# One FFN half of each kind, gate and up as a 2x2 block product of seven products

## Chip, cores and metric

The kernel runs on one core of one Trainium2 chip. The metric is device microseconds (us) of one execution; lower is better. The engines named below are TensorE (PE, with its weight loads as PEld), VectorE (DVE), ScalarE (ACT), GpSimd (POOL) and SyncE (SP), which issues most DMAs.

## What is computed

One decoder layer on 1024 tokens of width 1024 in float32: half a SwiGLU FFN, a mixer of two kinds of heads, half a SwiGLU FFN again, a final norm. Cut to what the change touches (D_FF is 2816 = 22 x 128):

```python
def rms_norm(x, g):
    return x * lax.rsqrt(jnp.mean(x * x, axis=-1, keepdims=True) + NORM_EPS) * g

def swiglu(h, w_gate, w_up, w_down):
    return (jax.nn.silu(h @ w_gate) * (h @ w_up)) @ w_down

x = x + 0.5 * swiglu(rms_norm(x, ffn1_norm), ffn1_w_gate, ffn1_w_up, ffn1_w_down)   # FFN1
x = x + hybrid_mixer(rms_norm(x, mix_norm), ...)
x = x + 0.5 * swiglu(rms_norm(x, ffn2_norm), ffn2_w_gate, ffn2_w_up, ffn2_w_down)   # FFN2
return rms_norm(x, final_norm)
```

## The kernel before

Tokens are cut into two halves of 512 (`TB`); activations lie feature-major, so that a tile is 128 features by 512 tokens. The order of the work is: FFN1 and the mixer's input projection of half 0 (`front`, L841), the mixer of half 0, FFN1 and input projection of half 1, the mixer of half 1, then for each half the output projection (`project_out`) and FFN2 (loop at L882 to L887). The mixer of a half is woven by the scheduler into the matmuls of what follows it. FFN1 of the first half runs before any mixer work exists, FFN2 of the second half after all of it.

**Precision.** A float32 product is made of three matmuls in the faster type fp32r: every operand is split into `hi` (a cast on ACT, L64) and `lo` (the rest, a subtraction on DVE, L65), and `mm3` (L89) adds hi x hi, hi x lo and lo x hi into one PSUM tile, per 128 rows of the contraction.

**FFN** (`ffn`, L172). `gain_split` (L153) makes the input h = x times the norm's gain, as eight hi/lo pairs `h_hi`, `h_lo`; the factor of the norm itself, r (`rs`), is computed beside the first products and multiplied in afterwards. The 22 columns of 128 gate and up weights are done in groups of 4, 4, 4, 4, 3, 3 (`GROUPS`). For each column `product` (L182) loads and splits the 1024x128 weights of gate, then of up, in two pieces of 128x512 each (`load_piece`, L69: DMA into `w_raw`, split into `w_hi`, `w_lo`), and runs 8 x 3 matmuls of 512 tokens into a PSUM tile. `gate` (L188) makes a = silu(gate r) r up: two products on DVE, silu on ACT, a product with the up tile on DVE, and a split into `a_hi`, `a_lo`. After each group the down products run (L230 to L235): for each of 8 output rows one piece of weights, 3 matmuls per column of the group, and an update of x on DVE. The first gate product of the next group is placed ahead of them (L229), so that PE has work while the last a is made.

In the second half of FFN2 the last group ends differently: `Finish` (L238) makes the down products token-major and goes straight on to the final norm and the output.

**What sets the order.** The program is written for a scheduler that places instructions on each engine's queue by priority and by readiness in its own model, and gives out buffers; every engine then works its queue in that order. What stands under `high_priority(AHEAD)` is drawn ahead: loads, splits, reads of PSUM. Buffers come from pools (L826 to L830), and a tile waits until the one that had its buffer is done: 5 raw weight tiles (`wraw`), 3 pairs of split weights (`whl`), 4 scratch tiles (`ft`); in PSUM 3 + 2 + 2 + 1 banks (`psf`, `hq`, `rq`, `ry`). The tiles `ra`, `bkt`, `uv` (pool `rw`) and `t4` belong to the mixer.

The input projection holds one place that the prediction uses: `tokens` (L313) multiplies with 256 columns at a time, with a new stationary operand for each matmul (L325 to L327).

Of the kernel before, what the change touches and what calls it, by code (L numbers as in the profile page):

```python
# [51 lines left out]
class Half:  # L52


    def __init__(self, hi, lo):
# [30 lines left out]
    return out  # L86


def mm3(E, ps, pairs, at=None, hook=None):  # L89
    n = len(pairs)  # L90
    for i, (w, x) in enumerate(pairs):
        if i == at:
            hook()
        E.nc.tensor.matmul(ps, w.hi, x.hi, start=(i == 0), stop=False)  # L94
        E.nc.tensor.matmul(ps, w.hi, x.lo, start=False, stop=False)  # L95
        E.nc.tensor.matmul(ps, w.lo, x.hi, start=False, stop=(i == n - 1))  # L96


def psum(E):
# [69 lines left out]
    return out  # L169


def ffn(E, xs, g, wgu, wdn, r=None, finish=None):  # L172
# [15 lines left out]
    def gate(pg, pu, half):  # L188
        with E.tc.high_priority(AHEAD):
            s = E.ft.tile([P, TB], F32, name="ft")  # L190
            if normed:
                nc.scalar.activation(out=s, in_=pg, func=AF.Silu)
            else:
                nc.vector.tensor_tensor(out=s, in0=pg, in1=r, op=ALU.mult)  # L194
                nc.scalar.activation(out=s, in_=s, func=AF.Silu)  # L195
                nc.vector.tensor_tensor(out=s, in0=s, in1=r, op=ALU.mult)  # L196
# [6 lines left out]
            return split(E, s, hi, lo)  # L203

    late = []
    for f0, nf in GROUPS:
# [23 lines left out]
        for d in range(KD):  # L230
            w = load_w(E, wdn[d, :, f0 * P:(f0 + nf) * P], nf)
            p = E.psf.tile([P, TB], F32, name="psf")
            mm3(E, p, list(zip(w, a)))
            with E.tc.high_priority(AHEAD):
                nc.vector.scalar_tensor_tensor(out=xs[d], in0=p, scalar=0.5, in1=xs[d], op0=ALU.mult, op1=ALU.add)  # L235
# [736 lines left out]
```

## Time and profile before

| what | value |
|---|---|
| median of 3 runs | 2111.35 us (2110.51 to 2111.99) |
| the profiled execution | 2111.92 us |
| its span, first to last instruction | 2109.9 us |
| first half of FFN1 in the span | about 7 to 373 us |
| second half of FFN2 in the span | about 1740 us to the end |
| instructions | 30312 |

The page of the profile gives, for each engine, busy time and its share of the span, and below it 40 slices of the span (52.7 us each) with the busy share of each engine in tenths. A group of instructions is shown by line, engine, operation and operands, with count, busy time and mean length. Matmuls and DVE instructions overlap their neighbours by some part, so lengths add up to more than the span; distances between starts do not have this flaw. For this reading, the slices of the two engines that the change loads:

```profile
DVE  7444445635888757766634788958784776444554
ACT  5223323626765445434626775546533553322333
```

Slices 1 to 7 are the first half of FFN1 and the last seven the second half of FFN2: DVE stands at 4 to 5 tenths there, ACT at 2 to 3, while the slices between, with the mixer woven in, reach 8 and 9 on DVE.

### The profile page before, as it was taken

What the parts mean: (1) busy time and instruction counts of PE and PEld (TensorE: products, weight loads), DVE (VectorE), ACT (ScalarE), POOL (GpSimd) and SP (SyncE); (2) the same over time, 40 slices, a digit from 0 to 9 for tenths busy, and PEclk for the clock granted to TensorE, in tenths of its full rate; (3) what the DMA queues carried; (4) which work ended last, traced back from release to release, by engine and by line L of the source; (5) the groups of instructions that cost most, each with busy time, mean ns of one, the idle gap of its engine ahead of it and who ended that gap; (6) DMA issues with size and microseconds to landing.
All of it is one profiled execution on the core that took longest, in us unless ns stands there. A gap on an engine that the chain in (4) does not pass through costs nothing.

```text
span 2109.9 us, 30312 instructions
## 1 busy us (share of the span) xinstructions
PE 2088.7 (99%) x11286; PEld 1698.6 (81%) x11286; DVE 1337.3 (63%) x2272; ACT 963.0 (46%) x1540; POOL 34.5 (2%) x68
## 2 busy tenths in 40 slices
PE   8999999999999999999999999999999999999998
PEld 6888888988888778877988878877787788888887
DVE  7444445635888757766634788958784776444554
ACT  5223323626765445434626775546533553322333
POOL 2000000010000000000000000000000000000000
PEclk9999999999999999999999999999999999999999
DMA  4333334544334423332644433423332453333332
GB/s 151 96 97 99 95 90 120 186 147 155 117 119 120 110 78 107 102 96 82 211 155 155 153 111 110 116 81 106 108 98 72 140 182 97 97 98 95 98 114 68
DMA packets 162724, 244.34 MB, mean 116 GB/s; under 512 B 37616, under 2 KB 57072, under 8 KB 162576
## 3 DMA queue, kind: packets, MB, share of 16 engines
q1 hardware_dynamic: 161712, 241.04, 38.4%
q8 instruction: 89, 1.46, 0.3%
q10 hardware_dynamic: 864, 1.36, 0.2%
q14 instruction: 59, 0.48, 0.1%
HBM read 210.35 MB, written 31.98 MB: 115 GB/s over the span
## 4 chain that ended last, share of the span: by engine, by line
PE 96%; DVE 1%; DMA 1%; issue 1%; ACT 1%; SPq 0%; DVEq 0%; ACTq 0%
PE psf L95 27%; PE psf L96 27%; PE psf L94 27%; PE rq L559 2%; PE rq L648 1%; PE hq L95 1%; PE hq L96 1%; PE hq L94 1%; PE rq L641 1%; PE rq L652 1%; PE ry L645 0%; DMA w_raw<-in_wgu_dram 0%; PE rq L639 0%; PE hq L485 0%; PE hq L478 0%
## 5 line engine op out<-in xcount | busy, mean ns | idle before, releaser
L64 ACT CAST w_hi<-w_raw 128x512 fp32r<-128x512 f32 (+2 forms) x696 | 420.5, 605 | 862.8 <-PE psf L95 763.8
L96 PE MATMUL psf<-h_hi,w_lo 128*128 128x512 f32 x1840 | 720.6, 392 | 0.5 <-DVE w_lo L65 0.5
L95 PE MATMUL psf<-h_lo,w_hi 128*128 128x512 f32 x1840 | 721.0, 392 | 0.0
L94 PE MATMUL psf<-h_hi,w_hi 128*128 128x512 f32 x1840 | 720.6, 392 | 0.3 <-ACT w_hi L64 0.3
L65 DVE TENSOR_TENSOR w_lo<-w_raw,w_hi 128x512 fp32r<-128x512 f32 (+2 forms) x696 | 460.9, 665 | 236.2 <-ACT w_hi L64 231.1
L96 PEld LDWEIGHTS psf<-h_hi,w_lo 128*128 128x128 f32 x1840 | 345.4, 188 | 73.6 <-DVE w_lo L65 1.5
L94 PEld LDWEIGHTS psf<-h_hi,w_hi 128*128 128x128 f32 x1840 | 345.5, 188 | 73.4 <-issue 1.2
L95 PEld LDWEIGHTS psf<-h_lo,w_hi 128*128 128x128 f32 x1840 | 345.4, 188 | 72.7 <-issue 0.7
L95 PE MATMUL psf<-a_lo,w_hi 128*128 128x512 f32 x680 | 268.3, 395 | 0.0
L96 PE MATMUL psf<-a_hi,w_lo 128*128 128x512 f32 x680 | 267.3, 393 | 0.0
L94 PE MATMUL psf<-a_hi,w_hi 128*128 128x512 f32 x680 | 266.7, 393 | 0.5 <-ACT a_hi L64 0.5
L235 DVE SCALAR_TENSOR_TENSOR x<-psf,x 128x512 f32<-128x512 f32 x184 | 126.1, 687 | 131.6 <-PE psf L96 130.9
L95 PEld LDWEIGHTS psf<-a_lo,w_hi 128*128 128x128 f32 x680 | 127.6, 188 | 28.1 <-issue 1.4
L94 PEld LDWEIGHTS psf<-a_hi,w_hi 128*128 128x128 f32 x680 | 127.6, 188 | 27.9 <-ACT a_hi L64 1.5
L96 PEld LDWEIGHTS psf<-a_hi,w_lo 128*128 128x128 f32 x680 | 127.7, 188 | 26.5 <-issue 0.5
L200 DVE TENSOR_TENSOR ft<-psf,ft 128x512 f32<-128x512 f32 x83 | 57.0, 687 | 71.3 <-PE psf L96 71.0
L194 DVE TENSOR_TENSOR ft<-psf,rs 128x512 f32<-128x512 f32 x64 | 44.1, 689 | 69.1 <-PE psf L96 69.0
L64 ACT CAST a_hi<-ft 128x512 fp32r<-128x512 f32 x88 | 54.5, 620 | 37.7 <-DVE ft L200 32.3
L65 DVE TENSOR_TENSOR a_lo<-ft,a_hi 128x512 fp32r<-128x512 f32 x88 | 60.3, 687 | 7.3 <-ACT a_hi L64 3.7
L386 DVE TENSOR_TENSOR ev<-psf,rs 128x512 f32<-128x512 f32 x44 | 30.3, 690 | 54.3 <-PE psf L96 54.3
L196 DVE TENSOR_TENSOR ft<-ft,rs 128x512 f32<-128x512 f32 x66 | 45.4, 691 | 8.4 <-ACT ft L195 4.6
L195 ACT ACTIVATE ft<-ft 128x512 f32<-128x512 f32 x66 | 41.5, 632 | 18.2 <-DVE ft L194 18.0
(332 smaller groups left out, 1966.7 us busy)
## 6 DMA issues: line engine op xcount, KB each, us to landing
w_raw<-in_wgu_dram SPq DMA_DIRECT2D x352, 256.0 KB, 3.1
w_raw<-in_wd_dram SPq DMA_DIRECT2D x134, 256.0 KB, 2.7
w_raw<-in_win_dram SPq DMA_DIRECT2D x96, 256.0 KB, 2.8
w_raw<-in_wd_dram SPq DMA_DIRECT2D x56, 192.0 KB, 2.3
w_raw<-in_wout_dram SPq DMA_DIRECT2D x32, 256.0 KB, 2.9
park<-x SPq DMA_DIRECT2D x16, 256.0 KB, 3.6
x<-park SPq DMA_DIRECT2D x16, 256.0 KB, 3.9
ft<-od SPq DMA_DIRECT2D x16, 256.0 KB, 3.3
```

The costliest lines, as they stand in the source:

```text
L64: nc.scalar.copy(out=hi, in_=raw)
L65: nc.vector.tensor_tensor(out=lo, in0=raw, in1=f32(hi), op=ALU.subtract)
L94: E.nc.tensor.matmul(ps, w.hi, x.hi, start=(i == 0), stop=False)
L95: E.nc.tensor.matmul(ps, w.hi, x.lo, start=False, stop=False)
L96: E.nc.tensor.matmul(ps, w.lo, x.hi, start=False, stop=(i == n - 1))
L194: nc.vector.tensor_tensor(out=s, in0=pg, in1=r, op=ALU.mult)
L195: nc.scalar.activation(out=s, in_=s, func=AF.Silu)
L196: nc.vector.tensor_tensor(out=s, in0=s, in1=r, op=ALU.mult)
L200: nc.vector.tensor_tensor(out=s, in0=pu, in1=s, op=ALU.mult)
L235: nc.vector.scalar_tensor_tensor(out=xs[d], in0=p, scalar=0.5, in1=xs[d], op0=ALU.mult, op1=ALU.add)
L386: nc.vector.tensor_tensor(out=e[:, 0:TB], in0=p, in1=r, op=ALU.mult)
L559: PE.matmul(gps[hh][:, c, :], bk[r, c0 + c, :, :], g.ra[r, jj, c0 + c, :, :], start=True, stop=True)
```

## The change

In the first half of FFN1 and in the second half of FFN2, columns 3 to 21 are no longer computed as two products over the whole contraction for 512 tokens. For each column the weights are taken as a 2x2 block matrix (rows: gate and up; columns: the first and the second four of the eight contraction tiles) and h as a 2x2 block matrix (rows: the same halves of the contraction; columns: tokens 0 to 255 and 256 to 511 of the half). The 2x2 product is made with seven block products in place of eight, each over 4 contraction tiles and 256 tokens, so 4 x 3 matmuls of 256 columns. Three columns go the old way first.

- `Versions` makes the right-hand factors. Three are parts of h; four more (t1 to t4) are sums and differences of parts, made in `make` for one pair of contraction tiles at a time (one ACT pass, one DVE pass, four DVE sums of 256, four splits), called twice in each of the first two `gate` calls. They lie in the mixer's tiles `ra`, `bkt`, `uv` and `t4`.
- `unit` is one column: four loads, the left-hand factors by four adds of 128x512 on POOL, and the seven products, each preceded by its split. Its PSUM tiles: x takes products 1, 3, 5 and 7, one upon another without being cleared; z takes product 2; y products 4 and 6.
- `Gate` reads the partial sums out of PSUM: three copies on ACT, three adds on DVE, then the steps of the old `gate`, the last product in two parts of 256.
- `units` runs two columns in turn, one product each, the second three products behind the first. Three products (`AFTER`) of the following columns stand between the end of a group and its down products.
- Groups are 3, 4, 4, 4, 4, 3. Pools: `wraw` 5 to 10, `ft` 4 to 6. The room comes from a smaller scratch area for dynamic DMAs, 1024.

```diff
+GROUPS_7 = ((0, 3), (3, 4), (7, 4), (11, 4), (15, 4), (19, 3))
+HK = KD // 2
+HT = TB // 2
+AFTER = 3
...
+class Versions:
+    def __init__(self, E, h):
+        self.of = {"11": [x[:, 0:HT] for x in h[:HK]], "21": [x[:, 0:HT] for x in h[HK:]], "22": [x[:, HT:TB] for x in h[HK:]]}
...
+    def make(self, E, xs, g, k):
+        nc = E.nc
+        V = nc.vector
+        with E.tc.high_priority(AHEAD):
+            a, b, p, q = (E.ft.tile([P, TB], F32, name="ft") for _ in range(4))
+            nc.scalar.activation(out=a, in_=xs[k], func=AF.Copy, scale=g[:, k:k + 1])
+            V.tensor_scalar(out=b, in0=xs[HK + k], scalar1=g[:, HK + k:HK + k + 1], scalar2=None, op0=ALU.mult)
+            t1, t3, t2, t4 = p[:, 0:HT], p[:, HT:TB], q[:, 0:HT], q[:, HT:TB]
+            V.tensor_tensor(out=t1, in0=a[:, HT:TB], in1=a[:, 0:HT], op=ALU.subtract)
+            V.tensor_tensor(out=t3, in0=b[:, HT:TB], in1=a[:, HT:TB], op=ALU.subtract)
+            V.tensor_tensor(out=t2, in0=b[:, HT:TB], in1=t1, op=ALU.subtract)
+            V.tensor_tensor(out=t4, in0=b[:, 0:HT], in1=t2, op=ALU.subtract)
+            for n, t in (("t1", t1), ("t3", t3), ("t2", t2), ("t4", t4)):
+                split(E, t, self.of[n][k].hi, self.of[n][k].lo)
...
+def unit(E, quads, v, use):
+    G = E.nc.gpsimd
+    def product(p, raw, n, start=True):
+        with E.tc.high_priority(AHEAD):
+            hi = E.whl.tile([P, 512], F32R, name="w_hi")
+            lo = E.whl.tile([P, 512], F32R, name="w_lo")
+            w = split(E, raw, hi, lo)
+        mm3(E, p, [(w[:, k * P:(k + 1) * P], v[n][k]) for k in range(HK)], start=start)
+    with E.tc.high_priority(AHEAD):
+        a11, a12, a21, a22, s1 = (E.wraw.tile([P, 512], F32, name="w_raw") for _ in range(5))
+        for t, q in zip((a11, a12, a21, a22), quads):
+            E.nc.sync.dma_start(out=t, in_=q)
+        G.tensor_tensor(out=s1, in0=a21, in1=a22, op=ALU.add)
+        G.tensor_tensor(out=a21, in0=a11, in1=a21, op=ALU.subtract)
+    x, z, y = (getattr(E, n).tile([P, TB], F32, name=n)[:, 0:HT] for n in ("hq", "psf", "rq"))
+    product(x, a11, "11")
+    use.m1(x)
+    with E.tc.high_priority(AHEAD):
+        G.tensor_tensor(out=a11, in0=s1, in1=a11, op=ALU.subtract)
+    yield
+    product(z, a12, "21")
+    use.m2(z)
+    with E.tc.high_priority(AHEAD):
+        G.tensor_tensor(out=a12, in0=a12, in1=a11, op=ALU.subtract)
+    yield
+    product(x, a11, "t2", False)
+    use.m6(x)
+    yield
+    product(y, s1, "t1")
+    use.m5(y)
+    yield
+    product(x, a21, "t3", False)
+    use.m7(x)
+    yield
+    product(y, a12, "22", False)
+    use.m3(y)
+    yield
+    product(x, a22, "t4", False)
+    use.m4(x)
...
+class Gate:
...
+    def m3(self, y):
+        E, V = self.E, self.E.nc.vector
+        self.add(self.t1, y)
+        with E.tc.high_priority(AHEAD):
+            V.tensor_tensor(out=self.t, in0=self.t, in1=self.r, op=ALU.mult)
+            E.nc.scalar.activation(out=self.t, in_=self.t, func=AF.Silu)
+            V.tensor_tensor(out=self.t, in0=self.t, in1=self.r, op=ALU.mult)
+    def m4(self, x):
+        E, V = self.E, self.E.nc.vector
+        s = 0.5 if self.half else 1.0
+        with E.tc.high_priority(AHEAD):
+            V.scalar_tensor_tensor(out=self.t0, in0=x, scalar=s, in1=self.t0, op0=ALU.mult, op1=ALU.mult)
+            V.scalar_tensor_tensor(out=self.t1, in0=self.u, scalar=s, in1=self.t1, op0=ALU.mult, op1=ALU.mult)
+            self.a = split(E, self.t, E.ap.tile([P, TB], F32R, name="a_hi"), E.ap.tile([P, TB], F32R, name="a_lo"))
...
+        begin()
+        for _ in range(3):
+            step()
+            yield
+        begin()
+        while lanes:
+            step()
+            yield
...
+    steps = units(nf)
+    for _ in range(AFTER):
+        next(steps)
+    down(a, f0, nf)
+    for f0, nf in groups[1:]:
+        last = finish and f0 + nf == NF
+        if last:
+            w_last = finish.weights(E, wdn, f0, nf)
+        while any(f not in done for f in range(f0, f0 + nf)):
+            next(steps)
+        a = [done[f] for f in range(f0, f0 + nf)]
+        if last:
+            finish(E, xs, a, w_last)
+            return
+        for _ in range(AFTER):
+            next(steps, None)
+        down(a, f0, nf)
...
-        nc=nc, tc=tc, const=pool("const", 1), wraw=pool("wraw", 5), whl=pool("whl", 3), ft=pool("ft", 4), rs=pool("rs", 2),
+        nc=nc, tc=tc, const=pool("const", 1), wraw=pool("wraw", 10), whl=pool("whl", 3), ft=pool("ft", 6), rs=pool("rs", 2),
...
-        ffn(E, xs, E.n1, wgu1, wd1, r)
+        ffn(E, xs, E.n1, wgu1, wd1, r, seven=b == 0)
...
-        ffn(E, xs, E.n2, wgu2, wd2, finish=Finish(nf_row, out_last) if b + 1 == NB else None)
+        ffn(E, xs, E.n2, wgu2, wd2, finish=Finish(nf_row, out_last) if b + 1 == NB else None, seven=b + 1 == NB)
...
-    nc = _bacc.Bacc("TRN2", target_bir_lowering=False, num_devices=1)
+    nc = _bacc.Bacc("TRN2", target_bir_lowering=False, num_devices=1, dynamic_dma_scratch_size=1024)
```

More of the change, by code (lines that the diff above doesn't have):

```diff
@@ L86, in load_w, with mm3 @@
     return out
-def mm3(E, ps, pairs, at=None, hook=None):
+def mm3(E, ps, pairs, at=None, hook=None, start=True):
     n = len(pairs)
+    on = dict(skip_group_check=not start)
     for i, (w, x) in enumerate(pairs):
@@ L93, in mm3 @@
             hook()
-        E.nc.tensor.matmul(ps, w.hi, x.hi, start=(i == 0), stop=False)
-        E.nc.tensor.matmul(ps, w.hi, x.lo, start=False, stop=False)
-        E.nc.tensor.matmul(ps, w.lo, x.hi, start=False, stop=(i == n - 1))
+        E.nc.tensor.matmul(ps, w.hi, x.hi, start=start and i == 0, stop=False, **on)
+        E.nc.tensor.matmul(ps, w.hi, x.lo, start=False, stop=False, **on)
+        E.nc.tensor.matmul(ps, w.lo, x.hi, start=False, stop=(i == n - 1), **on)
 def psum(E):
@@ new lines, with __init__, keep, add @@
+class Gate:
+    def __init__(self, E, r, half):
+        self.E, self.r, self.half = E, r, half
+        self.t, self.u = (E.ft.tile([P, TB], F32, name="ft") for _ in range(2))
+        self.t0, self.t1, self.u = self.t[:, 0:HT], self.t[:, HT:TB], self.u[:, 0:HT]
+    def keep(self, t, p):
+        with self.E.tc.high_priority(AHEAD):
+            self.E.nc.scalar.copy(out=t, in_=p)
+    def add(self, t, p):
+        with self.E.tc.high_priority(AHEAD):
+            self.E.nc.vector.tensor_tensor(out=t, in0=p, in1=t, op=ALU.add)
+    def m1(self, x):
+        self.keep(self.t0, x)
+    def m2(self, z):
+        self.add(self.t0, z)
+    def m6(self, x):
+        self.keep(self.t1, x)
+    def m5(self, y):
+        self.keep(self.u, y)
+    def m7(self, x):
+        self.add(self.u, x)
+    def m3(self, y):
[12 more added lines that the diff above has]
+            self.a = split(E, self.t, E.ap.tile([P, TB], F32R, name="a_hi"), E.ap.tile([P, TB], F32R, name="a_lo"))
@@ L173, in ffn @@
+def ffn(E, xs, g, wgu, wdn, r=None, finish=None, seven=False):
     nc = E.nc
     normed = r is not None
+    groups = GROUPS_7 if seven else GROUPS
     h = gain_split(E, xs, g, r)
     wait = bool(E.idle)
+    v = Versions(E, h) if seven else None
+    left = list(range(HK))
     def rms():
@@ L188, in gate @@
     def gate(pg, pu, half):
+        if seven and left:
+            v.make(E, xs, g, left.pop(0))
+            v.make(E, xs, g, left.pop(0))
         with E.tc.high_priority(AHEAD):
@@ L203, in gate, with down, units, begin @@
             return split(E, s, hi, lo)
+    def down(a, f0, nf):
+        for d in range(KD):
+            w = load_w(E, wdn[d, :, f0 * P:(f0 + nf) * P], nf)
+            p = E.psf.tile([P, TB], F32, name="psf")
+            mm3(E, p, list(zip(w, a)))
+            with E.tc.high_priority(AHEAD):
+                nc.vector.scalar_tensor_tensor(out=xs[d], in0=p, scalar=0.5, in1=xs[d], op0=ALU.mult, op1=ALU.add)
+    done = {}
+    def units(f0):
+        rest = list(range(f0, NF))
+        lanes = []
+        def begin():
+            if not rest:
+                return
+            f = rest.pop(0)
+            use = Gate(E, r, finish is not None and f >= groups[-1][0])
+            lanes.append((f, use, unit(E, [wgu[f, :, j, i * TB:(i + 1) * TB] for j in range(2) for i in range(2)], v, use)))
+        def step():
+            f, use, u = lanes.pop(0)
+            if next(u, True) is None:
+                lanes.append((f, use, u))
+                return
+            done[f] = use.a
+            begin()
[3 more added lines that the diff above has]
+            yield
+        begin()
+        while lanes:
+            step()
+            yield
     late = []
-    for f0, nf in GROUPS:
+    first = groups[:1] if seven else groups
+    for f0, nf in first:
         a = []
@@ L227, in ffn @@
             return
+        if seven:
+            break
         if f0 + nf < NF:
             late.append(product(f0 + nf, 0))
[L230 to L235, printed above, removed]
+        down(a, f0, nf)
+    if not seven:
+        return
+    steps = units(nf)
[11 more added lines that the diff above has]
+            finish(E, xs, a, w_last)
+            return
+        for _ in range(AFTER):
+            next(steps, None)
+        down(a, f0, nf)
 class Finish:
```

9 lines of the change are left out of this document (8 added, 1 removed).

## The prediction

> **What bounds the kernel now.** I read the busy shares first, then the granted clock in 40 slices, then the chain that ended last by engine. These are the three lines:
>
> ```profile
> PE 2088.7 (99%) x11286; PEld 1698.6 (81%) x11286; DVE 1337.3 (63%) x2272; ACT 963.0 (46%) x1540; POOL 34.5 (2%) x68
> PEclk9999999999999999999999999999999999999999
> PE 96%; DVE 1%; DMA 1%; issue 1%; ACT 1%; SPq 0%; DVEq 0%; ACTq 0%
> ```
>
> TensorE is busy for 99% of the span at full clock and is 96% of the chain. So I asked the waits (who waited for whom: us in total, times, longest), and one stretch inside the first half of FFN1 (us; PE, PEld, DVE, ACT, POOL busy; clock, DMA share, GB/s):
>
> ```profile
> PE hq L94 <- ACT h_hi L166: 6.9, 1, 6.9
> PE psf L96 <- DVE w_lo L65: 0.5, 1, 0.5
> ACT w_hi L64 <- PE psf L95: 763.8, 459, 3.8
> 210.00:300.00 90.00, 90.00 (x398) 74.51 (x397) 43.65 (x66) 27.65 (x45) 0.00 (x0) 1.00 0.33 97
> ```
>
> PE's longest wait is the start; for split weights it waited 0.5 us in all. It is ScalarE (ACT) that waits for PE to release a weight buffer: the three buffers are full ahead of PE. In the stretch VectorE (DVE) is 43.65/90 = 48% busy, ACT 31%, GpSimd (POOL) 0%. Only fewer or shorter matmuls can shorten these stages, as long as DVE keeps up.
>
> **What the change takes from PE.** A matmul's recorded length overlaps its neighbour's, so I take distances between starts (timeline: start, length, engine, line). Between the first two rows below lie 24 matmuls of 512 columns, between the second and the third 96 of 256 columns, each with its own weight load:
>
> ```profile
> 367.76 0.39 PE L94 MATMUL psf<-a_hi,w_hi 128*128 128x512 f32 x1
> ...
> 373.20 0.28 PE L325 MATMUL hq<-w_hi,h_hi 128*128 128x256 f32 x1
> ...
> 384.71 0.39 PE L145 MATMUL psf<-ft,ones_r 128*128 128x512 f32 x1
> ```
>
> That is 5.44/24 = 0.2267 us for 512 columns and 11.51/96 = 0.1199 us for 256, a little over half (0.1133). Gate and up of 128 columns cost 2 x 8 x 3 = 48 wide matmuls now, 10.88 us. A unit has 7 x 4 x 3 = 84 narrow ones, 10.07 us. So 12.5% fewer products leave 7.4% of PE's time: 0.81 us per unit. 22 - 3 = 19 units in each of two halves make 38: **-30.8 us**. The other columns, the down products (22 x 8 x 3 matmuls a half) and the other two halves keep their count. PE instructions rise by 38 x 36 = 1368.
>
> **What it adds on ACT and DVE.** Shapes kept apart (count | busy, mean ns), then two timeline rows of DVE back to back, with three more after them further down:
>
> ```profile
> L65 DVE TENSOR_TENSOR w_lo<-w_raw,w_hi 128x512 fp32r<-128x512 f32 x608 | 414.2, 684 | 214.9 <-ACT w_hi L64 211.6 <-DMA sh<-pd_q 0.9 <-ACT uv L649 0.6
> L65 DVE TENSOR_TENSOR w_lo<-w_raw,w_hi 128x256 fp32r<-128x256 f32 x16 | 6.7, 421 | 1.3 <-ACT w_hi L64 1.3
> L419 DVE TENSOR_SCALAR sh<-sh,lb,lb 128x512 f32<-128x512 f32 x8 | 4.3, 541 | 3.7 <-DMA sh<-pd_f 3.7
> L64 ACT CAST w_hi<-w_raw 128x512 fp32r<-128x512 f32 x608 | 376.9, 621 | 793.3 <-PE psf L95 716.0 <-issue 31.7 <-PE hq L95 9.7
> L333 ACT ACTIVATE ft<-hq,rt 128x256 f32<-128x256 f32 x8 | 3.1, 475 | 1.3 <-DVE rt L346 1.3
> L195 ACT ACTIVATE ft<-ft 128x512 f32<-128x512 f32 x66 | 41.5, 632 | 18.2 <-DVE ft L194 18.0
> 1438.34 0.69 DVE L674 TENSOR_TENSOR sr<-ra,sr 128x512 f32<-128x512 f32 x1
> ...
> 1440.75 0.69 DVE L679 TENSOR_TENSOR sr<-rq,sr 128x512 f32<-128x512 f32 x1
> ```
>
> Four DVE steps in 2.41 us: back to back one takes 0.60 of its 0.684 us, so a 256-column one about 0.421 - 0.08 = 0.34.
> - ACT per unit: 7 weight casts and the cast of a at 0.621, silu 0.632, three copies out of PSUM at 0.475 (the nearest row): 7.0 us of PE's 10.07. It fits.
> - DVE per unit: 7 w_lo, two products with r and a_lo at 0.60, three adds and two products of 256 columns at 0.34: 7.7 us (4.8 before, eight at 0.60). It fits too, alone.
> - Over four units and their eight down rows PE needs 4 x 10.07 + 96 x 0.2267 = 62.1 us (65.3 before), DVE 30.8 + 16 x 0.60 = 40.4.
>
> **What it adds on POOL,** where nothing like it ran: four adds of 128x512 per unit (L693 and the like are only clears). The nearest rows, and how POOL and DVE stand to each other (the POOL copy at 1439.75 lies between the DVE rows above):
>
> ```profile
> L774 POOL MEMSET sc<- 128x512 f32 x1 | 0.5, 531 | 0.1
> L769 POOL TENSOR_SCALAR_AFFINE_SELECT sh<-ones 64x256 f32<-64x256 f32 x2 | 0.8, 416 | 0.1
> L751 POOL TENSOR_SCALAR_AFFINE_SELECT ident<-ones 128x128 f32<-128x128 f32 x1 | 0.3, 287 | 0.0
> 1439.54 0.69 DVE L196 TENSOR_TENSOR ft<-ft,rs 128x512 f32<-128x512 f32 x1
> 1440.14 0.69 DVE L65 TENSOR_TENSOR w_lo<-w_raw,w_hi 128x512 fp32r<-128x512 f32 x1
> 1439.75 1.12 POOL L509 COPY sr<-carry 128x1 f32<-128x1 f32 x1 [16.65 <-DMA w_raw<-in_wgu_dram]
> 416.93 0.68 DVE L386 TENSOR_TENSOR ev<-hq,rs 128x512 f32<-128x512 f32 x1
> 417.67 0.18 POOL L390 COPY carry<-ev 128x1 f32<-128x1 f32 x1 [4.97 <-DVE ev L386]
> ```
>
> A clear, which reads nothing, is 0.53 us; one input costs (416 - 287)/128 = 1.0 ns a column on 0.16 fixed, so 0.67 us for 512. Two inputs lie between 0.67 (read side by side) and 0.16 + 2 x 0.516 = 1.19 (one after the other). I take 1.19, since a POOL that only passes data is already at 1 ns a column. A one-column copy takes 0.18 us; the one at 1439.75 ran until 1440.87, when the second DVE instruction with two SBUF inputs had ended (1440.83) and one reading PSUM (L679) had begun. So POOL waits whole DVE instructions out. That DVE waits likewise for POOL no row shows, since POOL never reads for long; I assume it, for the streaming part of 1.03 us. Each add then costs DVE 1.03, less 0.34 if it starts beside one of the four DVE steps of a unit that read PSUM: 0.69. Bounds: 0 (no exclusion) and 1.19 (nothing beside it).
>
> DVE per unit: 7.7 + 4 x 0.69 = 10.46 us against PE's 10.07; over the 62.1 us it all fits (40.4 + 16 x 1.03 = 56.9), but inside the units' own 40.3 us there are 41.8. Some three adds of sixteen, of the unit opened just before a down product, fall into the down rows: 41.8 - 2.1 = 39.7. So DVE is full, and queues form. After PE releases one of the three weight buffers it needs it again two products later, 2.88 us; cast and w_lo take 1.30; 1.58 are left. What stands ahead of w_lo in DVE's order: an add of PSUM and a product (0.34 + 0.60), or two half products and a_lo (1.28), and a POOL add (0.69): 1.63 and 1.97, over by 0.05 and 0.39. I take **0.3 us per unit, +11.4 us**; bounds 0 (free port) and 1.55 (12.5 us of DVE at 7.7 + 4 x 1.19, less three sixteenths of the adds, 0.89, against 10.07).
>
> [...]
>
> **The start of each half.** The four versions are made beside the first three columns: per pair one ACT pass, one tensor_scalar (0.54) and 8 DVE steps of 0.34, 3.3 us; four pairs 13.0 us of DVE, ahead of that stage's w_lo.
>
> ```profile
> 29.00:39.00 10.00, 10.00 (x46) 8.27 (x45) 9.43 (x15) 5.28 (x9) 0.00 (x0) 1.00 0.28 80
> 39.00:50.00 11.00, 11.00 (x51) 9.09 (x49) 6.47 (x11) 4.86 (x9) 0.00 (x0) 1.00 0.37 113
> 50.00:66.00 16.00, 16.00 (x72) 13.27 (x71) 8.19 (x13) 5.34 (x9) 0.00 (x0) 1.00 0.35 93
> 1752.00:1763.00 11.00, 11.00 (x50) 9.05 (x49) 8.25 (x9) 5.50 (x8) 0.00 (x0) 1.00 0.35 97
> ```
>
> DVE has 37 - 24.1 = 12.9 us free there, about what is asked. PE may wait between 0 and 6.5 us a half (half of it late); I take 3, **+6 us**.
>
> **At no cost.** The raw weights are the same 1 MB per unit, now four loads issued together on SP, with the down weights behind them in its queue:
>
> ```profile
> w_raw<-in_wgu_dram SPq DMA_DIRECT2D x352, 256.0 KB, 3.1
> ```
>
> Ten raw buffers are two units; the next unit's come free one by one from the old one's product 3 on, and its third product, the first that needs the sum on POOL, comes some 8.6 us after its last load can start (3.1 landing, 2.4 for two adds). If that cover is gone PE waits up to 3 us per unit. Product 3 writes the PSUM tile that ACT copies after product 1; with two units alternating, three products (4.3 us) lie between, against a copy of 0.475. Behind that matmul all of PE would wait. In the last units, with one alone, one product (1.44) remains: enough. The new copies and adds wait for PE's products, and behind them in the orders of ACT and DVE stand the casts and w_lo of the next products, for which PE waits; since they are ready the moment a product ends, as the old reads of PSUM were, this costs something only together with the bursts above. From the last product of a group's last unit to its a_lo it is 0.34 + 0.34 + 0.62 + 0.60 = 1.9 us on ACT and DVE; three steps of the next units (4.3 us) lie between, except in the last group of a half, where it was 0.60 + 0.62 + 0.60 before and stays so.
>
> **Sum.** -30.8 + 11.4 + 6 = -13.4. The profiled execution took 2111.92 us (span 2109.9 and 2.0 around it), 0.6 over the median: **2098.5 us**. About 0.2% (4.2 us) is what a measurement of this kernel can tell from no change.
>
> **Rivals.**
> - *All hidden.* POOL and DVE don't exclude each other, or the order spreads the adds; only 0 to 3 us a start remain: 2081 to 2087, say 2084. For it: the whole period has 56.9 of 62.1 us. Against: the copy of 1.12 us.
> - *Latency, no engine full.* The three weight buffers now last 2.88 us instead of 2 x 12 x 0.2267 = 5.44; two waits of 0.4 us per unit eat the gain: -30.8 + 38 x 0.8 + 6 = +5.6, about 2117. For it: the bursts of 1.63 and 1.97 against 1.58.
> - *The shared port bounds, slower.* If each add costs DVE its whole 1.19, a unit takes 7.7 + 4.76 - 0.89 = 11.6 us against 10.88 before: 38 x 0.7 + 6 = +33, about 2144. It decides from the point where an add costs DVE over (10.88 - 0.16 - 7.7)/4 = 0.75 us (0.16 is the start shared among 38), and I have taken 0.69. For it: POOL's copy waited for two DVE instructions; against: four of DVE's fifteen steps per unit, and all eight down updates of a group, read PSUM and leave the port free.
> - *It isn't half the time.* Narrow matmuls slower than 0.12: excluded by 96 of them in a row.
>
> **How the numbers follow.** Forecast (2090 to 2106) 0.40; all hidden 0.17; latency 0.15 (half of it within 0.2%, some of the forecast's upper edge too); port 0.28. Faster 0.57, same 0.12, slower 0.31. The range: up to 2138 leaves out the worst of the port (0.1), from 2084 the better half of all hidden (0.08). Cases of both signs hold much: the forecast's own range is 2090 to 2106.
>
> **What would show it.** Right: narrow matmuls 0.12 us apart; PE waits on w_lo (DVE) of some 0.3 us per unit; DVE near 100% in a stretch of units, and w_lo rows longer than 0.684 where POOL runs; POOL adds near 1.19 us; PE waits of 2 to 4 us about 40 and 1760 us. Wrong: w_lo at 0.684 beside POOL adds (no exclusion); PE waiting on ACT or DMA instead; PE waits longer in sum than 30.8 us.

## The result, and the profile after

| | before | after |
|---|---|---|
| median, four runs each | 2111.57 us (2110.51 to 2111.99) | 2164.51 us (2163.69 to 2166.63) |
| span of the profiled execution | 2109.9 us | 2162.2 us |

The change makes the kernel slower: ratio 1.0253, 95% interval 1.0235 to 1.0271. The forecast was 2098.5 us with a range of 2084 to 2138; the time lies 26.5 us above the range, beyond the rival "the shared port bounds" (2144).

From the profile's page of the changed kernel, the busy shares, two rows of the 40 slices (tenths) and the chain that ended last:

```profile
PE 2077.7 (96%) x12654; PEld 1744.0 (81%) x12654; DVE 1591.7 (74%) x2610; ACT 1066.5 (49%) x1806; POOL 261.2 (12%) x220
...
DVE  8878977744788757766634898967775787887786
...
POOL 2333432000000000000000000000000002343231
...
PE 83%; DVE 12%; DMA 2%; issue 2%; ACT 1%; SPq 0%; ACTq 0%; DVEq 0%
```

PE has 1368 more instructions, as counted, and 11 us less busy time, but the span is 52 us longer. POOL works in both halves with units; in the same slices DVE goes from 4 or 5 tenths to 7 or 8. DVE holds 12% of the chain, 1% before.

To see where, take starts of PE instructions (timeline). Before: first matmul of the fourth column, last matmul of this FFN half. After: the matmul behind PE's longest wait, still in the third column; the first matmul of a unit (after two such the third column goes on); the place from which the units run on; the start of four units in the middle; the down product behind them; the last matmul of the half.

```profile
46.60 0.39 PE L94 MATMUL psf<-h_hi,w_hi 128*128 128x512 f32 x1
...
372.98 0.39 PE L96 MATMUL psf<-a_hi,w_lo 128*128 128x512 f32 x1
```

```profile
46.15 0.80 PE L102 MATMUL psf<-h_hi,w_lo 128*128 128x512 f32 x1 [6.84 <-DVE w_lo L69]
...
54.80 0.38 PE L100 MATMUL hq<-h_hi,w_hi 128*128 128x256 f32 x1
...
62.10 0.28 PE L102 MATMUL hq<-h_hi,w_lo 128*128 128x256 f32 x1
...
224.04 0.28 PE L100 MATMUL psf<-h_hi,w_hi 128*128 128x256 f32 x1
...
270.21 0.40 PE L100 MATMUL psf<-a_hi,w_hi 128*128 128x512 f32 x1
...
399.15 0.39 PE L102 MATMUL psf<-a_hi,w_lo 128*128 128x512 f32 x1
```

The half ends 26.2 us later. The units run from 62.10 instead of 46.60: **15.5 us** late, predicted 3 (two of their matmuls are done by then). Four units then take 46.17 us, 11.54 each, against 10.88 for a column before. The remaining 10.7 us are the 19 units, a loss of 0.56 each on average; predicted was a gain of 0.51. The second half with units loses the other 26 us.

The same two places by windows (stretch, length; PE, PEld, DVE, ACT, POOL busy; clock, DMA share, GB/s): the start in three pieces, four units, their eight down rows.

```profile
29.00:39.00 10.00, 9.12 (x40) 6.86 (x38) 9.87 (x12) 8.58 (x15) 3.40 (x2) 1.00 0.09 22
39.00:50.00 11.00, 4.16 (x11) 3.08 (x10) 11.00 (x29) 7.32 (x16) 0.00 (x0) 0.64 0.13 37
50.00:62.00 12.00, 10.29 (x40) 7.92 (x40) 10.77 (x21) 4.26 (x9) 2.36 (x2) 0.90 0.11 33
224.04:270.21 46.17, 41.63 (x337) 40.31 (x336) 44.94 (x60) 24.39 (x48) 21.71 (x15) 1.00 0.27 87
270.21:292.01 21.80, 21.80 (x99) 18.03 (x97) 10.28 (x17) 4.99 (x8) 1.29 (x1) 1.00 0.35 108
```

At the start DVE is full for 21 us while PE is busy for 4.16 of 11 us, at a granted clock of 0.64. In the units DVE is busy for 44.94 of 46.17 us, 97%, and in the down rows behind them for 10.28 of 21.80. Fifteen of the sixteen adds lie in the units.

What PE waits for (us in total, times, longest), and DVE and POOL groups with shapes kept apart (count | busy, mean ns | idle before):

```profile
PE hq L100 <- DVE ft L298: 40.2, 34, 2.3
PE psf L102 <- DVE w_lo L69: 12.8, 5, 6.8
...
PE rq L102 <- DVE w_lo L69: 7.6, 12, 0.8
```

```profile
L69 DVE TENSOR_TENSOR w_lo<-w_raw,w_hi 128x512 fp32r<-128x512 f32 x722 | 574.8, 802 | 135.0 <-ACT w_hi L68 126.0 <-PE rq L710 2.3 <-PE psf L102 1.1
L292 DVE TENSOR_TENSOR ft<-ft,rs 128x512 f32<-128x512 f32 x38 | 42.1, 1107 | 1.8 <-ACT ft L291 0.7
L290 DVE TENSOR_TENSOR ft<-ft,rs 128x512 f32<-128x512 f32 x38 | 39.8, 1047 | 1.3
L269 DVE TENSOR_TENSOR ft<-psf,ft 128x256 f32<-128x256 f32 x38 | 15.8, 416 | 1.9 <-PE psf L102 0.8
```

The steps with two SBUF inputs have become longer (w_lo was 684 ns), the one that reads PSUM (L269, 416; 256 columns took 421 before) has not. The lengthening is (802 - 684) x 722 + (1107 - 684) x 38 + (1047 - 684) x 38 = 115 us: over 152 adds 0.76 us each. And PE's commonest wait is for L298, the DVE step that reads a unit's last product out of the PSUM tile x, which the first product of the unit after next is to overwrite. How one add gets there, in DVE, POOL and PE rows of the timeline:

```profile
113.92 0.69 DVE L290 TENSOR_TENSOR ft<-ft,rs 128x512 f32<-128x512 f32 x1
114.53 1.79 DVE L69 TENSOR_TENSOR w_lo<-w_raw,w_hi 128x512 fp32r<-128x512 f32 x1
116.24 1.77 DVE L292 TENSOR_TENSOR ft<-ft,rs 128x512 f32<-128x512 f32 x1
...
118.99 0.42 DVE L298 SCALAR_TENSOR_TENSOR ft<-hq,ft 128x256 f32<-128x256 f32 x1
...
114.21 1.56 POOL L226 TENSOR_TENSOR w_raw<-w_raw 128x512 f32<-128x512 f32 x1 [2.29 <-DMA w_raw<-in_wgu_dram]
115.85 1.62 POOL L227 TENSOR_TENSOR w_raw<-w_raw 128x512 f32<-128x512 f32 x1
...
119.56 0.36 PE L100 MATMUL hq<-h_hi,w_hi 128*128 128x256 f32 x1 [1.74 <-DVE ft L298]
```

The first add ends at 115.77; the split that began at 114.53 could only run then and ends at 116.32. The second add, begun at 115.85, was held by that split in turn and itself holds L292. L298 comes 2.2 us late, and PE stands for 1.74 us.

### The profile page after: what moved, and what is told of

It is laid out like the page before. It is cut to its first block, busy times and chain, and to the rows that moved or that the text cites. A ratio compares the mean times of both kernels' runs of the same rounds, so it can differ in the third digit from the quotient of the medians.

```text
span 2162.2 us, 34019 instructions
## 1 busy us (share of the span) xinstructions
PE 2077.7 (96%) x12654; PEld 1744.0 (81%) x12654; DVE 1591.7 (74%) x2610; ACT 1066.5 (49%) x1806; POOL 261.2 (12%) x220
## 3 DMA queue, kind: packets, MB, share of 16 engines
q8 instruction: 99, 1.62, 0.3%
## 4 chain that ended last, share of the span: by engine, by line
PE 83%; DVE 12%; DMA 2%; issue 2%; ACT 1%; SPq 0%; ACTq 0%; DVEq 0%
PE psf L101 20%; PE psf L100 20%; PE psf L102 20%; DVE w_lo L69 5%; PE hq L100 3%; PE hq L101 2%; PE hq L102 2%; DVE ft L292 2%; DVE ft L290 2%; PE rq L752 1%; PE rq L102 1%; PE rq L100 1%; PE rq L101 1%; PE rq L841 1%; DVE ft L269 1%
## 5 line engine op out<-in xcount | busy, mean ns | idle before, releaser
L68 ACT CAST w_hi<-w_raw 128x512 fp32r<-128x512 f32 (+3 forms) x810 | 489.3, 607 | 720.7 <-PE psf L101 558.9
L69 DVE TENSOR_TENSOR w_lo<-w_raw,w_hi 128x512 fp32r<-128x512 f32 (+3 forms) x810 | 623.1, 775 | 152.7 <-ACT w_hi L68 141.9
L102 PE MATMUL psf<-h_hi,w_lo 128*128 128x512 f32 (+1 forms) x1384 | 530.8, 384 | 12.4 <-DVE w_lo L69 12.4
L100 PE MATMUL psf<-h_hi,w_hi 128*128 128x512 f32 (+1 forms) x1384 | 531.2, 384 | 0.5 <-ACT w_hi L68 0.5
L101 PE MATMUL psf<-h_lo,w_hi 128*128 128x512 f32 (+1 forms) x1384 | 531.1, 384 | 0.0
L102 PEld LDWEIGHTS psf<-h_hi,w_lo 128*128 128x128 f32 x1384 | 261.9, 189 | 62.3 <-DVE w_lo L69 14.4
L100 PEld LDWEIGHTS psf<-h_hi,w_hi 128*128 128x128 f32 x1384 | 262.2, 189 | 51.4 <-issue 1.5
L101 PEld LDWEIGHTS psf<-h_lo,w_hi 128*128 128x128 f32 x1384 | 262.0, 189 | 49.7 <-issue 1.4
L100 PE MATMUL hq<-h_hi,w_hi 128*128 128x256 f32 (+1 forms) x216 | 72.3, 335 | 48.5 <-DVE ft L298 40.2
L226 POOL TENSOR_TENSOR w_raw<-w_raw 128x512 f32<-128x512 f32 x38 | 56.6, 1490 | 380.9 <-DVE ft L201 240.2
L237 POOL TENSOR_TENSOR w_raw<-w_raw 128x512 f32<-128x512 f32 x38 | 57.3, 1509 | 215.5 <-issue 118.5
```

The source lines that it names most:

```text
L68: nc.scalar.copy(out=hi, in_=raw)
L69: nc.vector.tensor_tensor(out=lo, in0=raw, in1=f32(hi), op=ALU.subtract)
L100: E.nc.tensor.matmul(ps, w.hi, x.hi, start=start and i == 0, stop=False, **on)
L101: E.nc.tensor.matmul(ps, w.hi, x.lo, start=False, stop=False, **on)
L226: G.tensor_tensor(out=s1, in0=a21, in1=a22, op=ALU.add)
L237: G.tensor_tensor(out=a12, in0=a12, in1=a11, op=ALU.subtract)
```

## The experiments

All are edits of the changed kernel. Where no ratio is given, a kernel ran once, beside one run of the kernel before on the same chip (2111.01 us for e1 to e4, 2110.78 for e7 to e10). Where a window of four units is quoted, it runs from the first unit after a row of down products to the next one.

### Is it the adds at all?

e1_no_add leaves the four adds out and multiplies raw blocks in place of the sums.

```diff
-        G.tensor_tensor(out=s1, in0=a21, in1=a22, op=ALU.add)
-        G.tensor_tensor(out=a21, in0=a11, in1=a21, op=ALU.subtract)
...
-        G.tensor_tensor(out=a11, in0=s1, in1=a11, op=ALU.subtract)
...
-        G.tensor_tensor(out=a12, in0=a12, in1=a11, op=ALU.subtract)
```

> The four adds on POOL are left out; each product that used a sum takes a raw block in its place, so the output is not the layer's. Theory A (shared port: the adds lengthen DVE's instructions by some 3 us per unit, and everything late follows from that): w_lo back to 0.684 us, a unit from 11.4 to 10.1 to 10.4 us, the wait for the x tile (40 us in all) nearly gone, time about 2164 - 38 x 1.2 = 2118. Theory B (the x tile in PSUM comes free too late whatever DVE's speed, since only two are in turn): that wait stays above 0.6 us per unit, and the time falls by less than 20 us.

2097.46 us. Four units by windows:

```profile
209.66:250.03 40.37, 40.37 (x337) 40.13 (x336) 34.85 (x60) 24.80 (x48) 0.00 (x0) 1.00 0.32 104
```

10.09 us a unit and PE never idle: the seven products cost what the prediction took (10.07), and the adds cost 46.17 - 40.37 = 5.8 us per four units, 1.45 per unit. For 38 units that is 55 of the 67 us by which the whole is shorter; 46 had been expected of the whole. With the same 60 DVE steps in the stage, DVE is busy for 34.85 us without adds and 44.94 with fifteen of them: 0.67 us of DVE per add. PE's longest wait for w_lo stays, so that has another cause (e3, below):

```profile
PE psf L102 <- DVE w_lo L69: 11.0, 5, 5.8
```

### Is it the lock, or waiting for the sums?

e9_adds_unread keeps four adds of the same size on POOL, but all of them write s1, which no product reads. e10_clears does the same with clears, which only write. In both, raw blocks stand in for the sums.

Here is one of the three other adds; e10 has `G.memset(s1, 0.0)` at all four places:

```diff
-        G.tensor_tensor(out=a21, in0=a11, in1=a21, op=ALU.subtract)
+        G.tensor_tensor(out=s1, in0=a21, in1=a22, op=ALU.add)
...
-    product(y, s1, "t1")
+    product(y, a22, "t1")
```

> As e1_no_add, but POOL makes four adds of 128x512 per unit at the same places, all of a21 + a22 into a tile that no product reads; the output is not the layer's. If the shared read port alone is the price, DVE's instructions are held up as in the changed kernel: w_lo near 0.80 us on average and 2150 to 2165 us. If it was the waiting for the sums, nothing waits for them here: 2097 to 2105.

> As e9_adds_unread, but POOL clears that tile four times per unit in place of the adds: it writes and reads nothing; the output is not the layer's. If the price is that of POOL's reads, w_lo stays at 0.684 and the time near 2097 to 2102. If any POOL work beside DVE costs, more than half of the loss comes back: over 2120.

e9: 2185.46 us; e10: 2099.47 us. Four units of e9, four of e10, and of e10 the split with the clear (by form):

```profile
231.61:281.80 50.19, 43.42 (x338) 41.89 (x337) 45.27 (x60) 24.37 (x48) 23.28 (x16) 0.97 0.28 90
```

```profile
210.63:250.98 40.35, 40.35 (x337) 40.13 (x336) 34.84 (x60) 24.83 (x48) 7.39 (x14) 1.00 0.32 105
```

```profile
L69 DVE TENSOR_TENSOR w_lo<-w_raw,w_hi 128x512 fp32r<-128x512 f32 x722 | 492.7, 685 | 139.1 <-ACT w_hi L68 120.8 <-PE rq L710 2.3 <-PE psf L102 1.1
```

```profile
L226 POOL MEMSET w_raw<- 128x512 f32 x38 | 20.1, 528 | 779.6 <-DVE w_lo L69 539.8 <-DMA w_raw<-in_wgu_dram 239.8
```

Nobody waits for e9's sums, and its units are as long as the changed kernel's or longer. Clears at the same places, 0.53 us each, leave w_lo at 685 ns and cost next to nothing (2.0 us over e1, one run each); they keep the fifth raw tile too, so e1 didn't gain by its room. So the price comes from POOL's reading beside DVE, not from the lateness of a sum. The rows of the changed kernel show the hold in both directions: w_lo goes from 0.69 to 1.79 us behind an add (114.53), an add from 1.28 to 1.62 us behind w_lo (115.85).

e9 is slower still, beyond what was expected. There the four adds of a unit run in one burst: POOL was idle for 3.0 us in all ahead of each of the last three groups of 38, in the changed kernel for 123.5 and 215.5 us ahead of the last two (L232, L237). That the burst is the reason was not tested.

### The adds on DVE instead

e4_dve_adds moves the four adds to the engine that they hold up. e8_third_dve also takes x from three PSUM tiles in turn (the edit of e2, below).

```diff
-    G = E.nc.gpsimd
+    G = E.nc.vector
```

> The same four adds per unit on DVE in place of POOL: 4 x 0.60 = 2.4 us of DVE work per unit in place of some 3.0 us in which DVE stands blocked. Theory A: DVE per unit 10.1 us, a unit 10.5 to 11.2, time 2130 to 2155. Theory B: no gain, since the chain that frees x has the same steps and DVE more to do: 2160 to 2185.

> The adds on DVE, and a third PSUM tile for x. With the adds on DVE, PE still waited 6.6 us for x and nothing else in the units: theory A with the x wait as a second, smaller bound gives 2115 - 6 = 2109; if DVE is full the wait moves to w_lo and the time stays at 2113 to 2117.

2115.26 and 2108.63 us, the first below all that was expected of it. The four units of e4, all but the ten last of their 336 matmuls (1.18 us, placed among the down rows):

```profile
212.32:252.38 40.06, 39.69 (x328) 38.89 (x327) 39.00 (x73) 23.86 (x46) 0.00 (x0) 1.00 0.30 98
```

10.3 us a unit. DVE has 13 more steps in the stage than in e1 and is still busy for only 39.00 us. A 512-column step takes it 0.60 us back to back; the same add on POOL cost it 0.67 by e1's window and 0.76 by the lengths. On the idle engine the add is dearer for the full one. Like against like the gap is wider: by the same difference of windows an add on DVE costs (39.00 - 34.85)/13 = 0.32 us, since DVE's steps then run closer together than in e1.

### Where the delay shows: the PSUM tile

```diff
-    x, z, y = (getattr(E, n).tile([P, TB], F32, name=n)[:, 0:HT] for n in ("hq", "psf", "rq"))
+    E.turn = getattr(E, "turn", -1) + 1
+    x, z, y = (getattr(E, n).tile([P, TB], F32, name=n)[:, 0:HT] for n in (("hq", "hq", "ry")[E.turn % 3], "psf", "rq"))
```

> Nothing but a third PSUM tile for x (hq, hq, ry in turn). Theory B: the wait of a unit's first product for DVE's last read of x (40 us in all) goes and nothing comes in its place: about 2125. Theory A: DVE is full, so the wait moves to w_lo: 2145 to 2160.

2159.35 us. PE's waits:

```profile
PE hq L102 <- DVE w_lo L69: 19.5, 36, 1.1
...
PE ry L102 <- DVE w_lo L69: 9.3, 19, 1.1
```

The wait for L298 is gone and PE waits for w_lo instead; four units take 46.43 us. Taken alone, the tile is where the delay shows, not its cause (e20, below, has more on it).

### Two adds of four

e15_two_two puts the last two adds on DVE, e16_last_two_pool the first two.

One add of each pair, e15's first:

```diff
-        G.tensor_tensor(out=a11, in0=s1, in1=a11, op=ALU.subtract)
+        E.nc.vector.tensor_tensor(out=a11, in0=s1, in1=a11, op=ALU.subtract)
```

```diff
-        G.tensor_tensor(out=s1, in0=a21, in1=a22, op=ALU.add)
+        E.nc.vector.tensor_tensor(out=s1, in0=a21, in1=a22, op=ALU.add)
```

> Two of a unit's four adds (the two made while the unit runs) on VectorE, two left on GpSimd. Known: no adds 10.09 us a unit, four on VectorE 10.3, four on GpSimd 11.55; whole runs 2097.46, 2115.26 and 2164.51. Theory 'each GpSimd add holds VectorE by itself, so the price goes by their number': halfway, 10.8 to 11.1 us a unit, 2135 to 2145. Rival 'VectorE is only just full with four, below that its free time takes the holds in': 10.2 to 10.5 us a unit, 2113 to 2122.

> The mirror of e15: the first two adds of a unit on VectorE, the two made while the unit runs on GpSimd. In e15 a unit took 11.39 us and VectorE's two-input steps were held for 0.79 us per GpSimd add. Theory 'the place decides: the first pair falls on the product with r and the split ahead of the read that frees the PSUM tile, the last pair on splits that are made early': 10.3 to 10.7 us a unit, 2115 to 2130, VectorE still held by about 0.7 us per add. Rival 'the hold costs the same wherever it falls': 11.2 to 11.5 us a unit, 2147 to 2157, as e15.

e15: 2153.59 us, ratio 1.0207 (1.0190 to 1.0224). e16: 2172.44 us, ratio 1.0292 (1.0275 to 1.0309). Four units of e15, four of e16; then the wait that leads e16's list, and one such case in its DVE, POOL and PE rows:

```profile
223.65:269.34 45.69, 41.62 (x337) 40.30 (x336) 43.64 (x67) 24.39 (x48) 11.70 (x8) 1.00 0.27 90
```

```profile
224.06:271.04 46.98, 41.85 (x337) 40.41 (x336) 42.27 (x68) 24.76 (x48) 11.42 (x7) 1.00 0.27 91
```

```profile
PE hq L102 <- DVE w_lo L69: 34.6, 31, 1.8
```

```profile
162.18 1.75 DVE L69 TENSOR_TENSOR w_lo<-w_raw,w_hi 128x512 fp32r<-128x512 f32 x1
...
161.70 1.68 POOL L232 TENSOR_TENSOR w_raw<-w_raw 128x512 f32<-128x512 f32 x1 [8.55 <-DVE w_lo L69]
...
163.97 0.38 PE L102 MATMUL hq<-uv,w_lo 128*128 128x256 f32 x1 [0.78 <-DVE w_lo L69]
```

No expectation of the two runs held: 11.4 and 11.7 us a unit, and two adds about as dear as four. For e15 DVE's load gives a reason: seven more steps in the stage (67 for 60) add 7 x 0.60 = 4.2 us, and seven holds fewer (8 adds for 15) take 7 x 0.67 = 4.7 away; it stays 96% busy. For e16 that doesn't do, since DVE is 90% busy. Its holds are a little shorter too: w_lo is 735 ns on average, the second part of the last product (L299, 256 columns of two SBUF inputs) 762 for 421, and the products with r are back at 684, which makes ((735 - 684) x 722 + (762 - 421) x 38) / 76 = 0.66 us per add. In the case shown the split for which PE waits is itself the one that is held. So a full DVE isn't the whole of it: a hold seems to be paid also where the held step is the next that PE needs.

### How much room lies between DVE and PE

Three pairs of split weights lie ahead of PE. e17_four_split has four pairs, at the price of two raw weight tiles; e18_eight_raw gives up the raw tiles alone.

The edit of e17 (e18 keeps 3 in `whl`):

```diff
-wraw=pool("wraw", 10), whl=pool("whl", 3)
+wraw=pool("wraw", 8), whl=pool("whl", 4)
```

> The changed kernel with four pairs of split weights instead of three (room for it from eight raw weight tiles instead of ten, which e18 changes alone). In the changed kernel VectorE is 91% busy in the units (45.37 of 50 us) and a unit takes 11.55 us. Theory 'a held split is late because only three pairs are ahead of TensorE (latency)': with a fourth the units come down to VectorE's own time, 10.5 to 10.8 us, total 2125 to 2140. Rival 'the loss is not in the depth of the split weights (VectorE's order, the sums, the PSUM tiles)': 11.3 to 11.6 us a unit, 2155 to 2168.

> The changed kernel with eight raw weight tiles instead of ten, the control for e17. If a unit's loads are early enough with eight: within 4 us of 2164.51. If the sums then come later: up to 2185, and e17 is read against this run instead.

2301.61 us, ratio 1.0917 (1.0860 to 1.0974), and 2261.49 us, ratio 1.0717 (1.0700 to 1.0734). The control lost 97 us by itself; its first two waits, now for weights:

```profile
PE psf L100 <- ACT w_hi L68: 54.8, 58, 2.6
PE psf L102 <- DVE w_lo L69: 41.4, 34, 5.3
```

So e17 can't answer. e19_five_split and e20_five_third find room elsewhere: as in e3 (below) the four versions aren't made, and two more pairs lie in the tile `ra`. e20 has e2's three x tiles as well.

```diff
+        self.more = [(ra[:, i * 1024:i * 1024 + 512], ra[:, i * 1024 + 512:(i + 1) * 1024]) for i in range(2)]
...
+            v.turn = (v.turn + 1) % 5
+            if v.turn < 2:
+                hi, lo = v.more[v.turn]
+            else:
+                hi = E.whl.tile([P, 512], F32R, name="w_hi")
+                lo = E.whl.tile([P, 512], F32R, name="w_lo")
```

> e3 (versions not made, 2144.40, 11.57 us a unit) with five pairs of split weights for the units instead of three: two more lie in a tile that the versions would have used. Theory 'latency through three pairs': the units come down to VectorE's own time, 10.5 to 10.8 us, total 2108 to 2120. Rival 'the sums and VectorE's own order set the pace': 11.3 to 11.6 us, 2138 to 2147.

> e19 with x in three PSUM tiles in turn, as e2. If the weights' buffers and x together hold the units (each hides behind the other): 10.3 to 10.8 us a unit, 2105 to 2120, though e19 and e2 alone change little. If the sums and VectorE's order set the pace: 11.3 to 11.6 us, 2138 to 2147 again.

e19: 2140.23 us, ratio 1.0139 (1.0122 to 1.0156), beside 2144.40 for e3. e20: 2117.68 us, ratio 1.0032 (1.0020 to 1.0044). Four units and their down rows, e3, then e20:

```profile
212.19:258.47 46.28, 41.97 (x337) 40.65 (x336) 44.93 (x60) 24.39 (x48) 21.72 (x15) 1.00 0.26 86
258.47:280.26 21.79, 21.79 (x98) 18.03 (x97) 10.33 (x17) 4.99 (x8) 1.29 (x1) 1.00 0.35 108
```

```profile
206.97:248.76 41.79, 41.23 (x338) 40.28 (x336) 40.76 (x55) 21.25 (x43) 19.33 (x14) 1.00 0.28 90
248.76:272.51 23.75, 22.05 (x98) 17.95 (x97) 14.60 (x22) 7.21 (x14) 3.84 (x3) 1.00 0.34 109
```

More pairs alone change little (45.71 us per four units), a third x alone as little (46.43); both together bring the units to 10.45 us. Each hid behind the other. The rows show what the room does: five of the 60 DVE steps and an add or two move into the down rows, where DVE has time. In the units DVE stays the full engine (98%). The down rows lose 2 us of it again.

### The start

Five kernels. e3_no_versions doesn't make the four versions (a part of h stands in for them). The others keep e8's edits: e7 makes the versions at low priority; e11 also begins with four columns the old way, makes no versions beside the first two and two pairs beside each of the next two, and puts two products of the units, not three, ahead of the first down rows; e12 is e11 at high priority; e13 is e11 with one pair beside each of the four columns.

The edit of e11 in `make`, the groups, `gate` and ahead of the first down rows:

```diff
-        with E.tc.high_priority(AHEAD):
+        with E.tc.high_priority(0):
...
-GROUPS_7 = ((0, 3), (3, 4), (7, 4), (11, 4), (15, 4), (19, 3))
+GROUPS_7 = GROUPS
...
-        if seven and left:
+        calls.append(0)
+        if seven and len(calls) > 2 and left:
...
-    for _ in range(AFTER):
+    for _ in range(2):
```

> The four versions of h are not made; the products that use them take part 22 of h, so the output is not the layer's. Theory C (the making of the versions, drawn ahead of the weights' splits, costs 15 us in the first half and as much in the second): 2164 - 30 = 2134, first unit of FFN1 begins near 47 us instead of 62. Rival: the start is late for another reason (loads, cold clock), and the time falls by less than 12 us.

> As e8_third_dve, and the versions of h are made without being drawn ahead of the weights' splits. Theory C (order at the start): PE's wait for w_lo at 46 us (5.7 to 6.8 us) and the cold clock behind it go, 8 to 12 us in the first half, a few in the second: 2094 to 2102. Rival: DVE's load there is the price whatever its order, and the start is at most 4 us shorter.

> As e8 (adds on VectorE, x in three tiles in turn, 2108.63), and the start spread out: a first group of 4 columns the old way, no versions beside its first two, two pairs beside the third and the fourth, 2 products (not 3) of the units ahead of the first down products, versions at low priority. 18 units a half. Theory 'the start is lost because VectorE has no room beside the first columns': the 5 to 12 us waits of TensorE for w_lo at about 45 us shrink to 0 to 3 in all, the first half of FFN1 ends at about 361 to 363 us (373.0 before), total 2086 to 2092. Rival 'the versions cost their whole VectorE time wherever they stand, or the hand-over into the units stalls by itself': the waits only move to about 55 us, the half ends at 370 to 375, total 2104 to 2110.

> As e11 but with the versions made at high priority, as in the changed kernel. Theory 'VectorE's load at the start': the place is what counts, so within 3 us of e11. Rival 'their priority, ahead of w_lo, is what stalls TensorE': waits of 3 us or more for w_lo return at about 50 us, and it is 5 us or more above e11.

> As e11 but one pair of versions beside each of the four first columns. Theory 'VectorE's load': the first two columns also carry the norm and the split of h, so VectorE still has no room there: waits for w_lo of 2 to 5 us a half, 3 to 8 us above e11. Rival 'only the number of pairs per column counts': at or below e11.

| | us | ratio to before |
|---|---|---|
| e3_no_versions | 2144.40 | one run |
| e7_third_dve_low | 2107.13 | one run |
| e11_later_low | 2094.44 | 0.9921 (0.9906 to 0.9936) |
| e12_later | 2102.99 | 0.9963 (0.9951 to 0.9975) |
| e13_one_low | 2096.24 | 0.9929 (0.9914 to 0.9944) |

Without the versions the whole gains 20 us where 30 were expected, 11.6 of them in the first half (by the first matmul behind it, at 387.83 instead of 399.38), and the first unit starts at 49.84 instead of 62.10:

```profile
49.84 0.28 PE L100 MATMUL hq<-h_hi,w_hi 128*128 128x256 f32 x1
```
Low priority at the crowded place gained 1.5 us over e8, no more than single runs differ by, where 2094 to 2102 us in all was expected; the later place with it gained 14.2. Before, DVE's load up to the end of the third column, and in e11 the stretch in which the versions are now made:

```profile
29.00:46.60 17.60, 17.60 (x80) 14.55 (x78) 13.91 (x22) 8.28 (x13) 0.00 (x0) 1.00 0.32 95
```

```profile
39.00:50.00 11.00, 11.00 (x51) 9.09 (x50) 10.84 (x22) 8.12 (x15) 0.00 (x0) 1.00 0.29 90
50.00:62.00 12.00, 12.00 (x64) 10.32 (x62) 12.00 (x27) 7.15 (x16) 0.00 (x0) 1.00 0.17 49
```

DVE is as full as it was, but PE works all the time and the clock stays at 1.00. e12, with the same places and the old priority, is 8.6 us slower, where 3 at most were expected; its waits for w_lo into psf come to 6.1 us, in e11 to 1.0 (e12 first):

```profile
PE psf L102 <- DVE w_lo L69: 6.1, 4, 2.7
```

```profile
PE psf L102 <- DVE w_lo L69: 1.0, 2, 0.7
```

So the expectation that place alone counts failed there: place and order both do. e13, 1.8 us above e11 where 3 to 8 were expected, shows that even one pair per column nearly fits if it goes last in line. e11 is the fastest kernel of this study, 16.3 us under the kernel before, 70 under the changed one, 2.4 us above what was expected of it.

## Why the prediction was wrong

**What bounds the kernel, and PE's gain: right.** 10.07 us was taken for a unit without hindrance; e1 has 10.09. The -30.8 us are there to be had, and e11 has a good half of them.

**The price of an add: near the truth.** 0.69 us of DVE was taken: 1.03 us in which an add of 1.19 streams, less 0.34 beside a PSUM step. The add is longer, 1.28 us unhindered (119.22) and 1.34 to 1.62 by group means (L232, L227); with 1.28 the same working gives 0.78. The units' steps that read PSUM weren't held (L269 and L298, 413 to 422 ns), and the hold is 0.67 us (windows, e1) to 0.76 (lengths). That DVE waits for POOL, which was assumed, is shown by w_lo: 1.79 us behind an add, 685 ns on average beside the clears of e10.

**The step that failed: "DVE is full, and queues form ... I take 0.3 us per unit, +11.4 us".** The load inside the units was put at 39.7 us for PE's 40.3, just under the edge; it is 44.94. Back to back the steps need the 30.8 us that were taken. But fifteen adds lie in the units, where thirteen were put, and hold DVE for 0.76 us each, not 0.69: 11.4 us where 8.9 stood. The last 2.7 us I put down to steps that don't run back to back (0.684 for 0.60); no run measured that alone. In e4, with POOL idle and DVE as full, 73 steps come to 39.00 us where 30.8 + 13 x 0.60 = 38.6 would stand, so there they do run back to back. With DVE 97% busy and its work kept in the units by the buffers (e20), the unit goes at DVE's pace, not at PE's plus a queue: measured +1.45 us a unit over e1 where 0.3 stood. In the first half the forecast missed by 19 x (0.56 + 0.51) = 20.4 us in the units and by 12.5 us at the start.

The rival "the shared port bounds" had the hold, and by luck nearly the size, 11.6 us against 11.54; that a port is behind it no run shows. It put an add at 1.19 us of DVE, where 0.67 to 0.76 were measured. With 0.76 and fifteen adds its own sum gives 7.7 + 11.4/4 = 10.55 us a unit, a gain. Too low in it, as in the forecast, are DVE's own steps between the holds (the 2.7 us above, 0.7 a unit) and the 46.17 - 44.94 = 1.2 us in which DVE stands. The upper bound of 1.55 us per unit comes to 1.50 from its own terms (12.46 - 0.89 - 10.07); the measured 11.54 - 10.07 = 1.47 lies just inside it.

**"At no cost": one place was overlooked.** The working checked that product 3 could write x after the copy of product 1, and not that the first product of the unit after next must wait until L298 has read the tile. It became PE's commonest wait (40.2 us). By e2 it costs little by itself (5 us, one run), but by e20 it and the three pairs of split weights together hold the units up: 10.45 us a unit with both loosened, part of DVE's work then lying in the down rows.

**The second step that failed: "DVE has 37 - 24.1 = 12.9 us free there, about what is asked ... I take 3".** The free time was read from the stage of four columns up to 66 us. After the change the units begin after three, so only what lies before 46.60 counts: 17.6 - 13.91 = 3.7 us, for 13.0 asked. That leaves 9.3 us late by this count, beyond the bound of 6.5. Of the other 6 of the 15.5 us, 3.0 are slow matmuls behind the long wait: the 15 from 46.15 to 52.56, at a granted clock of 0.52, take 6.41 us, and 3.40 at 0.2267 each. The two adds drawn ahead into the start (3.40 us of POOL in 29 to 39) cost some 1.5: without adds (e1) the units run from 60.64 instead of 62.10. The rest, under 2 us, stays open. The prediction had it as +6 for both halves; the versions alone cost 20 by e3.

**The waits foretold:** PE waits for w_lo (DVE) and long ones at 40 us came (6.84 us, for 2 to 4 foretold); so did a full DVE and w_lo rows over 0.684. A sign of "wrong" came as well: PE's waits exceed 30.8 us in sum, since the three rows shown alone make 60.6. "All hidden" fell with the holds. "Latency, no engine full" fell with DVE at 97%, but the weight buffers that it named do count, together with x (e20).

**Left open:** why two adds cost about as much as four. e15 has a reason in DVE's load, e16 only in part. A mix of fewer adds on POOL with more room was not tried.

## What to carry to other kernels

Look at what an idle GpSimd costs beside VectorE: in the changed kernel a two-input add on it took 0.67 to 0.76 us of VectorE's time, more than the 0.60 of a VectorE step of that size back to back. Sum an engine's load over the stretch in which the work can really lie, with the buffers as they are, and count as free only time that is still free after the change. When one wait is removed and another takes its place at the same total, look for the pair: e2 and e19 each gained 4 or 5 us, both edits together 27.

## What the hardware showed that was not expected

- Adds whose results nobody reads held up the kernel more than those in use: 2185.46 us (e9, one run) against 2164.51.
- Two adds on GpSimd back to back held two DVE steps in a row, at 1.79 and 1.77 us for 0.69: the second add started at 115.85 behind a split that the first had held, and took 1.62 for 1.28 us.
- PE's long stall was paid twice: behind the wait of 6.84 us matmuls of 512 columns stood 0.43 us apart for some 6 us, instead of 0.2267, and the granted clock of that stretch (46.15 to 52.56) was 0.52. Behind the wait of 1.68 us, at 56.98, they were back at 0.23 after one.
